# An encoder trunk with its first stage reordered, and the ALiBi bias applied by a scale in the softmax step

## The chip, the cores and the metric

One core of a Trainium2 chip runs the whole program. The metric is device time in microseconds, the median of the runs; all times below are microseconds (us) unless marked otherwise. PE is TensorE's matmuls, PEld its weight loads, DVE is VectorE, ACT is ScalarE, POOL is GpSimd, SP is SyncE, which here issues nearly all transfers.

## What is computed

Two layers over 512 tokens of width 1024. Each layer normalises the tokens with a scale and a shift from the conditioning vector, projects them (three dilated groups for 8 heads, a low-rank "latent" group for 8 more), runs dilated attention with ALiBi and latent attention, and then an MLP:

```python
c_act = jax.nn.silu(c)
for l in range(DEPTH):
    mod = c_act @ w_mod[l] + b_mod[l]
    sh1, sc1, gt1, sh2, sc2, gt2 = jnp.split(mod, 6, axis=-1)
    h = rms_norm(x, g_norm_mix[l]) * (1.0 + sc1[:, None]) + sh1[:, None]
    q_d, k_d, v_d, cq, ckv, k_rope = jnp.split(h @ w_in[l], cuts, axis=-1)
    q_d = rms_norm(q_d ..., g_q_dil[l]);  k_d = rms_norm(k_d ..., g_k_dil[l])
    o_dil = dilated_attention(q_d, k_d, v_d, positions, slopes)   # three windows, mixed
    o_mla = latent_attention(cq, ckv, k_rope, positions, ...)
    x = x + gt1[:, None] * (jnp.concatenate([o_dil, o_mla], axis=-1) @ w_out[l])
    h = rms_norm(x, g_norm_mlp[l]) * (1.0 + sc2[:, None]) + sh2[:, None]
    x = x + gt2[:, None] * (jnp.square(jax.nn.relu(h @ w_mlp_in[l])) @ w_mlp_out[l])

# inside each dilated window (dist = |pos_q - pos_k|, slope of head h = 2 ** -(h + 1)):
s = einsum(q, k) * Dh ** -0.5 - slopes * dist
s = where(mask, s, -1e30)
```

The kernel forms the three windows of a dilated head as one dense softmax over 512 keys: score plus a bias, where the bias is slope x |distance| plus a mask table of logarithms (`lnc`), both with their sign turned, so that the step takes a minimum.

## The kernel before

Every product runs in three matmuls of split operands (`mm3`: high x high, low x high, high x low). A weight tile is loaded by SP into `raw` (3 buffers) or `zz` (2 buffers), its high part is copied by ACT (L233) and its low part subtracted by POOL (L234). The tokens are tiled in eight feature tiles k (128 features by 512 tokens) and four token blocks tb.

The **first stage** (L734 to L793) makes the first projections. The 16 modulation blocks that it needs are loaded as 128x1024 weight tiles and multiplied on DVE with the broadcast conditioning vector `cb`, summing along the row (L170). The squares of x are added on DVE, summed by a matmul with ones (L753, `ones`), and turned into the inverse root `y` (`inv_rms`). Then, for each tile k: DVE multiplies x by the root into u (L759; L768 for the first), ACT makes the high half `h` (L772) and the full value (L773), and POOL or DVE the low half (L775, L763). PE takes for each tile the dilated group's 384 columns of all four token blocks and the latent group's 416 columns of all four. DVE's list alone is written out by hand there (`manual_schedule`); the others' orders come from the scheduler. Behind the loop stand the chains (squares L451, inverse roots, scaling L469), the transposes, the latent group's tail and rotary tables, and the distances (L327):

```python
for tb in range(4):
    W["do_chain"](tb, lbanks[tb])
for fn in PR[0]["tail"]:
    fn()
W["tail"]()
bias0 = distances()
```

Eight **stages** `st` follow, each with a pair of heads: 0 to 3 dilated, 4 to 7 latent. While the heads of one pair run (scores L492 and L493, softmax step L350, exponential, normalisation, transposes L365, values L377), `weave` puts the matmuls of the next pair's projections between them, each event at a position of the `TUNE` table. In layer 0 a dilated head makes its bias for each query block: ACT takes the absolute value of the signed distance times the slope (L345), POOL adds the mask table g (L346), SP stores it to HBM for layer 1, and DVE's softmax step adds it to the score:

```python
A.activation(b, dist[qb // 2][:, qb % 2], AF.Abs, scale=SLOPES[h])
G.tensor_tensor(b, b, g[:, 384 - 128 * qb:896 - 128 * qb], op=OP.add)
V.tensor_tensor_reduce(P, sc, b, op0=OP.add, op1=OP.min, scale=1.0, ...)
```

Names in the rows: `mm`, `sc`, `tr` are PSUM banks (4, 2 and 2 buffers); `qk`, `ot`, `pt`, `h`, `wh`, `wl`, `raw`, `zz`, `P`, `b`, `s`, `o` are SBUF buffers of a pool of that name; `kcol` and `mcol` are columns that scale keys.

## Time and profile before

| | us |
|---|---|
| runs | 1343.17, 1344.11, 1348.12; median 1344.11 |
| the profiled execution | 1343.71, its span 1341.6 |
| PE busy | 1263.8 (94%) |
| DVE, ACT, POOL busy | 762.4, 679.8, 652.0 |
| mean granted TensorE clock | 0.984 |

The profile follows one execution instruction by instruction. A timeline row gives the start, the duration, the engine, the line, the operation with output and inputs, and behind it in brackets how long the engine had been idle and what ended that. A row of grouped instructions gives busy time and the mean duration in ns. The granted clock is the share of full speed that TensorE had.

### The profile page before, as it was taken

The page shows a single profiled execution, that of the slowest core. Times are in us where ns is not written, and L with a number is a line of the kernel's source. Part 1 is how long each engine was busy: PE and PEld are TensorE (multiplying, and loading weights), DVE is VectorE, ACT ScalarE, POOL GpSimd, SP SyncE. Part 2 cuts the span into 40 slices and gives each one's busy share as a digit, 9 for nine tenths or more (in the row PEclk, how much of TensorE's full clock was granted, in tenths as well). Part 3 has the DMA queues.
Part 4 walks back from the last instruction along what each step waited for, and adds up shares of the span by engine and source line. Part 5 has one row for each costly group of instructions (what it writes and reads, how often), then busy time and mean ns, then how long its engine had stood idle before and what let it go on. Part 6 is the DMA issues. An engine that isn't in the chain of part 4 may idle for free.

```text
span 1341.6 us, 19641 instructions
## 1 busy us (share of the span) xinstructions
PE 1263.8 (94%) x7114; PEld 1108.2 (83%) x7114; DVE 762.4 (57%) x1644; ACT 679.8 (51%) x1421; POOL 652.0 (49%) x504
## 2 busy tenths in 40 slices
PE   4879988988999999999999999899899999999998
PEld 2878867877998888888899999798799888888888
DVE  6777797886763661834476678987672121121223
ACT  5567898777632322322237677887663232232321
POOL 5646876674534444444438333545452444444441
PEclk7989999999999999999999999999999999999999
DMA  9335543332254572844434244211121222232221
GB/s 340 113 100 174 184 156 110 105 122 69 79 176 166 192 250 95 278 166 161 166 121 131 77 135 123 86 48 63 40 72 64 95 95 96 96 106 96 94 95 64
DMA packets 57248, 167.62 MB, mean 125 GB/s; under 512 B 8640, under 2 KB 10816, under 8 KB 57152
## 3 DMA queue, kind: packets, MB, share of 16 engines
q1 hardware_dynamic: 57152, 166.38, 37.2%
q8 instruction: 56, 0.92, 0.3%
q14 instruction: 40, 0.33, 0.1%
HBM read 155.87 MB, written 10.49 MB: 124 GB/s over the span
## 4 chain that ended last, share of the span: by engine, by line
PE 75%; DVE 6%; ACT 5%; DMA 3%; POOL 3%; issue 2%; DVEq 0%; ACTq 0%; POOLq 0%
PE mm L241 22%; PE mm L244 22%; PE mm L245 22%; PE tr L377 3%; PE tr L365 2%; DMA raw<-in_wout_dram 1%; DVE pt L371 1%; POOL wl L234 1%; DVE P L350 1%; ACT P L354 1%; PE sc L241 1%; ACT wh L233 1%; POOL raw L167 1%; PE sc L244 1%; PE sc L492 1%
## 5 line engine op out<-in xcount | busy, mean ns | idle before, releaser
L234 POOL TENSOR_TENSOR wl<-raw,wh 128x1024 fp32r<-128x1024 f32 (+3 forms) x174 | 395.2, 2273 | 434.4 <-ACT wh L233 431.1
L233 ACT ACTIVATE wh<-raw 128x1024 fp32r<-128x1024 f32 (+3 forms) x174 | 174.7, 1004 | 264.7 <-PE mm L245 212.0
L670 DVE SCALAR_TENSOR_TENSOR x<-mm,mod,x 128x512 f32<-128x512 f32 (+1 forms) x152 | 92.4, 621 | 255.1 <-PE mm L245 254.5
L241 PE MATMUL mm<-h,wh 128*128 128x512 f32 (+1 forms) x544 | 198.3, 364 | 0.0
L244 PE MATMUL mm<-h,wl 128*128 128x512 f32 (+1 forms) x544 | 198.1, 364 | 0.0
L245 PE MATMUL mm<-h,wh 128*128 128x512 f32 (+1 forms) x544 | 197.9, 364 | 0.0
L241 PE MATMUL mm<-ot,wh 128*128 128x512 f32 (+1 forms) x416 | 147.1, 354 | 0.8 <-DVE x L670 0.4
L865 ACT ACTIVATE P<-mm 128x512 f32<-128x512 f32 (+1 forms) x80 | 41.0, 513 | 210.3 <-PE mm L245 206.8
L245 PE MATMUL mm<-ot,wh 128*128 128x512 f32 (+1 forms) x416 | 143.7, 349 | 1.5 <-POOL ot L663 1.5
L244 PE MATMUL mm<-ot,wl 128*128 128x512 f32 (+1 forms) x416 | 144.9, 349 | 0.0
L866 DVE SCALAR_TENSOR_TENSOR mm<-mm,P 128x512 f32<-128x512 f32 (+1 forms) x80 | 46.9, 589 | 135.7 <-ACT P L865 135.7
L241 PEld LDWEIGHTS mm<-h,wh 128*128 128x128 f32 x544 | 102.7, 189 | 16.3
L244 PEld LDWEIGHTS mm<-h,wl 128*128 128x128 f32 x544 | 102.7, 189 | 16.1
L245 PEld LDWEIGHTS mm<-h,wh 128*128 128x128 f32 x544 | 102.6, 189 | 16.2
L241 PE MATMUL mm<-qk,wh 128*128 128x512 f32 (+1 forms) x288 | 105.3, 366 | 1.0 <-DVE x L670 1.0
L244 PE MATMUL mm<-qk,wl 128*128 128x512 f32 (+1 forms) x288 | 105.3, 365 | 0.0
L245 PE MATMUL mm<-qk,wh 128*128 128x512 f32 (+1 forms) x288 | 105.2, 365 | 0.0
L170 DVE SCALAR_TENSOR_TENSOR pt<-pt,cb 128x1024 f32<-128x1024 f32 x56 | 100.7, 1828 | 0.0
L371 DVE TENSOR_TENSOR pt<-tr,pt 128x512 fp32r<-128x512 f32 x128 | 86.6, 684 | 18.1 <-ACT pt L370 17.5
L362 POOL TENSOR_SCALAR P<-P,hs 128x512 f32<-128x512 f32 x64 | 48.1, 751 | 99.9 <-DVE hs L355 81.0
L241 PE MATMUL mm<-wh,h 128*128 128x384 f32 x240 | 81.3, 353 | 11.7 <-ACT h L772 9.8
L365 PE MATMUL tr<-ident,P 128*128 128x128 f32 x512 | 77.5, 275 | 15.7 <-DVE o L381 6.1
(290 smaller groups left out, 2968.9 us busy)
## 6 DMA issues: line engine op xcount, KB each, us to landing
raw<-in_w_dram SPq DMA_DIRECT2D x64, 512.0 KB, 3.4
pt<-in_wmod_dram SPq DMA_DIRECT2D x56, 512.0 KB, 4.8
raw<-in_w2a_dram SPq DMA_DIRECT2D x48, 512.0 KB, 3.5
raw<-in_wmod_dram SPq DMA_DIRECT2D x24, 512.0 KB, 3.6
raw<-in_win_dram SPq DMA_DIRECT2D x30, 384.0 KB, 3.0
bias<-b SPq DMA_DIRECT2D x32, 256.0 KB, 2.1
raw<-in_wout_dram SPq DMA_DIRECT2D x16, 512.0 KB, 3.7
raw<-in_w2b_dram SPq DMA_DIRECT2D x16, 512.0 KB, 3.4
```

The costliest lines, as they stand in the source:

```text
L170: r = V.scalar_tensor_tensor(w, w, 1.0, cb, op0=OP.mult, op1=OP.mult, accum_out=out)
L233: ra = A.activation(hi, raw, AF.Copy)
L234: rg = G.tensor_tensor(lo, raw, f(hi), op=OP.subtract)
L241: r = T.matmul(out, sh, mh, start=first, stop=False)
L244: T.matmul(out, sl, mh, start=False, stop=False)
L245: T.matmul(out, sh, ml, start=False, stop=last)
L362: G.tensor_scalar(P, P, r_, 0.0, op0=OP.mult, op1=OP.add)
L365: T.transpose(tr[:, kc], P[:, kc * 128:(kc + 1) * 128], ident)
L371: V.tensor_tensor(lo, tr, f(hi), op=OP.subtract)
L670: V.scalar_tensor_tensor(xT[j][:, hf], p, gt[:, j:j + 1], xT[j][:, hf], op0=OP.mult, op1=OP.add)
L865: A.activation(r, p, AF.Relu)
L866: V.scalar_tensor_tensor(p, p, 0.0, r, op0=OP.max, op1=OP.mult)
```

## The change

It has three parts.

- **First stage.** c and the positions are loaded as rows and turned by PE. The squares are added in pairs by DVE for six tiles and not at all for two; five matmuls with ones accumulate the sum in PSUM. The broadcast of the conditioning vector stays in PSUM (`cbp`), and each modulation block is multiplied in two halves of 512. The small steps that make a tile's scale and shift go from ACT to DVE. POOL makes all eight low halves. The orders of SP, DVE, ACT and POOL are written out by hand.
- **Latent group.** In the k loop PE takes only the dilated group. The latent weights' second pair of tiles is loaded last (`late`); token blocks 0 and 1 are multiplied behind the dilated banks, blocks 2 and 3 inside the first stage of heads. The rotary tables move into stage 1, with the sine table and the reload of the exponential's table around the k loop.
- **Slope.** |distance| is made once, unscaled. Keys are multiplied by 1/slope (a small DVE step on the key's inverse root, `isl`), the mask table g is doubled in place by ACT at the start of every layer-0 dilated head (head h has half the slope of the one before it), and the softmax step multiplies the sum with the slope.

```diff
+    isl = col(8, "isl")
+    for h in range(8):
+        V.memset(isl[:, h:h + 1], 1.0 / SLOPES[h])
...
     def first_norm(j):
-        A.activation(modc[0][:, j:j + 1], mraw[:, j:j + 1], AF.Identity, bias=...)
-        A.activation(amix[0][:, j:j + 1], mraw[:, 8 + j:9 + j], AF.Identity, bias=gb0[:, j:j + 1], scale=...)
+        V.scalar_tensor_tensor(modc[0][:, j:j + 1], mraw[:, 0, j:j + 1], ..., mraw[:, 1, j:j + 1], op0=OP.add, op1=OP.add)
+        V.tensor_tensor(msum, mraw[:, 0, 8 + j:9 + j], mraw[:, 1, 8 + j:9 + j], op=OP.add)
+        V.scalar_tensor_tensor(amix[0][:, j:j + 1], msum, ..., gb0[:, j:j + 1], op0=OP.mult, op1=OP.add)
...
-    def inv_rms(p, v, y, t):
+    def inv_rms(p, v, t):
+        A.activation(t, p, AF.Ln, bias=epsc, scale=1.0 / D)
         V.tensor_scalar(v, p, 1.0 / D, EPS, op0=OP.mult, op1=OP.add)
-        A.activation(t, v, AF.Ln)
         A.activation(p, t, AF.Exp, scale=-0.5)
...
+    def distances(low):
         for qb in range(4):
             d = dist[qb // 2][:, qb % 2]
-            A.activation(d, row[:, 0], AF.Identity, bias=clm[:, 0, qb:qb + 1], scale=65536.0)
-            V.scalar_tensor_tensor(d, row[:, 1], clm[:, 1, qb:qb + 1], d, op0=OP.subtract, op1=OP.add)
+            if low:
+                V.scalar_tensor_tensor(d, rowf[:, 1], clm[:, 1, qb:qb + 1], d, op0=OP.subtract, op1=OP.add)
+                A.activation(d, d, AF.Abs)
+            else:
+                G.tensor_scalar(d, rowf[:, 0], 65536.0, clm[:, 0, qb:qb + 1], op0=OP.mult, op1=OP.add)
...
     def head(l, h, hd, score, bias, vals, o, hook=lambda at: None):
         pt = ...
+        if bias and l == 0:
+            A.activation(bias[1], bias[1], AF.Copy, scale=2.0)
...
-                    A.activation(b, dist[qb // 2][:, qb % 2], AF.Abs, scale=SLOPES[h])
-                    G.tensor_tensor(b, b, g[:, 384 - 128 * qb:896 - 128 * qb], op=OP.add)
+                    G.tensor_tensor(b, dist[qb // 2][:, qb % 2], g[:, 384 - 128 * qb:896 - 128 * qb], op=OP.add)
...
-                V.tensor_tensor_reduce(P, sc, b, op0=OP.add, op1=OP.min, scale=1.0, scalar=3e38, accum_out=m)
+                V.tensor_tensor_reduce(P, sc, b, op0=OP.add, op1=OP.min, scale=SLOPES[h], scalar=3e38, accum_out=m)
...
                     rs = rsqrt_tiny(v, 4 * nb, bank)
+                    rk = rs.rearrange("p (n k d) -> p n k d", k=2, d=2)[:, :, 1]
+                    V.tensor_tensor(rk, rk, isl[:, 2 * pr:2 * pr + 2]...to_broadcast([128, nb, 2]), op=OP.mult)
...
+            def late(i):
+                wr[4 + i] = load(a["winc"][0, i], 2 * W_C, ("raw", "zz")[i % 2])
+            def late_split(i):
+                W["put"](i, *split(wr[4 + i], 2 * W_C, ("ot", "ot") if i < 2 else ("wh", "wl")))
+            def mod_mul(i):
+                for w in range(2):
+                    c = slice(512 * w, 512 * w + 512)
+                    V.scalar_tensor_tensor(ml[i][:, c], ml[i][:, c], 1.0, cbp[w], ..., accum_out=mraw[:, w, i:i + 1])
+            with tc.manual_schedule(engines={E.SP, E.DVE, E.Activation, E.Pool}):
+                for k in range(8):
+                    mods(k)
+                    if k % 2 == 0:
+                        weights(k // 2)
+                    if k > 3:
+                        late(k - 4)
...
+                distances(False)
...
+                for k in range(8):
...
+                    V.tensor_tensor(u, xT[k], p, op=OP.mult)
+                    A.activation(hi, u, AF.Identity, bias=be, scale=ga)
+                    A.activation(u, u, AF.Identity, bias=be, scale=ga)
+                    G.tensor_tensor(lo, u, f(hi), op=OP.subtract)
+                    if k % 2 == 0 and k < 6:
+                        PR[0]["put"](k // 2 + 1, *split(wr[k // 2 + 1], 768))
                     if k < 7:
+                        mod_mul(9 + k)
+                        mod_mul(k + 1)
                         first_norm(k + 1)
+                    if k > 5:
+                        late_split(k - 6)
+                    for tb in range(4):
+                        PR[0]["step"](banks[tb][:, :384], k, tb)
...
             for tb in range(4):
                 PR[0]["do_chain"](tb, banks[tb])
+            gains()
+            for i in (2, 3):
+                late_split(i)
+            lbanks = {0: ps("sc")}
+            for k in range(8):
+                W["step"](lbanks[0][:, :W_C], k, 0, pin=k == 0)
+            distances(True)
...
+            if l == 0 and st == 0:
+                for tb in (2, 3):
+                    ev += spread(W["mm"][tb], 1.2 * tb - 2.4, 1.2 * tb - 1.3) + [(1.2 * tb - 1.25, W["chain"][tb])]
+                ev += [(2.5, W["tail"])] + flow(nx, 2.6, 7.6) + [(5.2, nx["tail"][0]), (8.8, nx["tail"][1])]
...
+            if l == 0 and st == 1:
+                ev += [(2, W["rope"])]
```

The order moves on several engines. On SP, in the first stage before, `winc` tiles (latent weights) come between modulation blocks (`wmod`) and the next pair's `win`:

```order
L165 DMA qk_495<-in_wmod_dram 128x1024
L165 DMA ot_499<-in_wmod_dram 128x1024
L232 DMA raw_404<-in_winc_dram 128x832
L506 DMA gr_730<-in_gqr_dram 128x32
L793 DMA cols_71<-in_cols_dram 128x71
L232 DMA raw_603<-in_win_dram 128x768
```

After, the last four `winc` tiles of the stage close the list of loads, and the fourth, `zz_227`, takes the buffer of the second, `zz_213`:

```order
L256 DMA zz_213<-in_winc_dram 128x832
L172 DMA qk_215<-in_wmod_dram 128x1024
L172 DMA qk_217<-in_wmod_dram 128x1024
L256 DMA zz_219<-in_win_dram 128x768
L256 DMA raw_221<-in_winc_dram 128x832
L172 DMA qk_223<-in_wmod_dram 128x1024
L172 DMA qk_225<-in_wmod_dram 128x1024
L256 DMA zz_227<-in_winc_dram 128x832
```

All latent weights are thus loaded late, the fourth last. On ACT, behind the eighth tile's value, before, there stands one weight copy (of the second pair) and then the squares and value copies of the dilated banks:

```order
L773 ACTIVATE pt_201<-pt_201,mod_167,am_169 128x512
L233 ACTIVATE wh_610<-raw_609 128x768
L451 ACTIVATE s_566<-mm_202 128x256
L457 ACTIVATE qk_564<-mm_202 128x2x64
L451 ACTIVATE s_566<-mm_203 128x256
L457 ACTIVATE qk_564<-mm_203 128x2x64
```

After, there stand three latent weight copies, a table load and four absolute values (the distances `ot_162` and `ot_163`) ahead of the same squares:

```order
L831 ACTIVATE pt_178<-pt_178,mod_143,am_145 128x512
L247 ACTIVATE ot_482<-zz_213 128x832
L112 ACT_TABLE_LOAD
L247 ACTIVATE wh_555<-raw_221 128x832
L247 ACTIVATE wh_559<-zz_227 128x832
L350 ACTIVATE ot_162<-ot_162 128x512 x2
L350 ACTIVATE ot_163<-ot_163 128x512 x2
L477 ACTIVATE s_511<-mm_279 128x256
```

The copy of `zz_227`, the last tile loaded, moved ahead of the squares. On PE, the first score of the first pair (`sc_785`), before, is followed by the next pair's projection (384 columns, `mm_819`):

```order
L547 MATMUL mm_722<-ident,zz_616 128x128
L492 MATMUL sc_785<-qk_562,qk_561 128x512
L493 MATMUL sc_785<-qk_563,qk_561 128x512
L241 MATMUL mm_819<-wh_604,h_184 128x384
L244 MATMUL mm_819<-wh_604,h_185 128x384
L245 MATMUL mm_819<-wl_605,h_184 128x384
```

After, the latent group's 416 columns of token block 2 (`mm_732`) stand around the two halves of that score:

```order
L521 MATMUL sc_699<-qk_507,qk_506 128x512
L265 MATMUL mm_732<-ot_462,h_164 128x416
L268 MATMUL mm_732<-ot_462,h_165 128x416
L269 MATMUL mm_732<-ot_463,h_164 128x416
L265 MATMUL mm_732<-ot_462,h_164 128x416
L268 MATMUL mm_732<-ot_462,h_165 128x416
L269 MATMUL mm_732<-ot_463,h_164 128x416
L522 MATMUL sc_699<-qk_508,qk_506 128x512
```

The latent transposes (L547) and the projection of the second pair stand further down.

More of the change, by code (lines that the diff above doesn't have):

```diff
@@ L146, in trunk @@
[L146 to L154 removed]
+        T.matmul(cbp[i], ones, dg.rearrange("p k c -> p (k c)"), start=True, stop=True)
@@ new lines, in trunk @@
+    sines = const.tile([128, 2, 4, 16], F32, name="sines")
+    sin, cos = sines[:, 0], sines[:, 1]
+    clm = const.tile([128, 3, 4], F32, name="clm")
+    parts = s2([4, 3, 128], tag="b")
+    V.tensor_copy(parts[:, 2], prow)
+    V.tensor_scalar(pi[:, 0], prow, 16, None, op0=OP.arith_shift_right)
+    V.tensor_scalar(pi[:, 1], prow, 65535, None, op0=OP.bitwise_and)
+    V.tensor_copy(parts[:, :2], pi)
+    turn = ps("sc")
+    for i in range(3):
+        T.transpose(turn[:, 4 * i:4 * i + 4], parts[:, i], ident[:4, :4])
@@ L238, in load_split, with load @@
         return hi, lo
+    def load(src, n, raw="raw", keep=False):
+        raw = t4(raw, [128, 1024], F32)[:, :n]
+        r = SY.dma_start(raw, src)
+        if keep:
+            tc.keep_in_program_order(r)
+        return raw
+    def load_split(src, n, keep=False, tags=("wh", "wl")):
+        return split(load(src, n, keep=keep), n, tags, keep=keep)
     def mm3(out, sh, sl, mh, ml, first, last, pin=False):
```

254 lines of the change are left out of this document (124 added, 130 removed).

## Prediction

> **What bounds the kernel now.** I read the page's table of busy tenths, then the busy time by stretches cut at the events that matter, then the timeline around those cuts.
>
> ```profile
> PE   4879988988999999999999999899899999999998
> ```
>
> ```profile
> 0.00:25.73 25.73, 5.86 (x6) 1.68 (x6) 14.81 (x43) 14.43 (x25) 11.55 (x20) 0.74 0.89 320
> 25.73:70.30 44.57, 39.82 (x192) 37.39 (x192) 33.71 (x46) 24.75 (x46) 28.67 (x23) 0.92 0.45 167
> 70.30:94.70 24.40, 17.46 (x77) 15.69 (x76) 19.86 (x52) 14.77 (x54) 6.75 (x8) 0.79 0.29 86
> 94.70:127.60 32.90, 30.02 (x187) 27.82 (x186) 24.61 (x61) 25.30 (x57) 23.82 (x17) 1.00 0.57 181
> 127.60:157.50 29.90, 28.07 (x171) 26.66 (x170) 25.05 (x60) 25.54 (x56) 23.93 (x17) 0.94 0.53 173
> 157.50:187.80 30.30, 28.02 (x186) 25.52 (x184) 26.39 (x66) 25.46 (x63) 19.90 (x17) 1.00 0.47 155
> 187.80:215.90 28.10, 20.66 (x130) 16.31 (x129) 18.94 (x56) 23.55 (x56) 25.98 (x28) 0.88 0.53 171
> ```
>
> The first row is PE in 40 slices of the span. Behind each stretch stand its length, then the busy time of PE, PEld, DVE, ACT and POOL, the granted clock, the DMA share and GB/s. After 216 us PE stands at nines and eights, so time can only come out of PE's idle or slow-clock time ahead of that: the first stage (to 94.7, the first softmax), and the four dilated stages behind it. The events of the first stage:
>
> ```profile
> 14.17 2.08 PE L753 MATMUL sc<-o,ones 128*128 128x512 f32 x2 [5.35 <-DVE o L128]
> 24.14 0.69 DVE L768 TENSOR_TENSOR pt<-x,P 128x512 f32<-128x512 f32 x1
> 53.26 0.62 PE L244 MATMUL mm<-wh,h 128*128 128x384 f32 x1 [1.87 <-POOL h L775]
> 54.00 0.52 PE L244 MATMUL mm<-wh,h 128*128 128x384 f32 x1
> 54.32 0.52 PE L245 MATMUL mm<-wl,h 128*128 128x384 f32 x1
> 56.62 0.43 PE L241 MATMUL sc<-wh,h 128*128 128x416 f32 x1
> 59.73 0.35 PE L241 MATMUL tr<-wh,h 128*128 128x416 f32 x1
> 59.79 0.81 ACT L772 ACTIVATE h<-pt,mod,am 128x512 fp32r<-128x512 f32 x1
> 59.91 0.35 PE L244 MATMUL tr<-wh,h 128*128 128x416 f32 x1
> 67.95 0.38 ACT L451 ACTIVATE s<-mm 128x256 f32<-128x256 f32 x1 [5.75 <-PE mm L245]
> 70.38 0.36 ACT L222 ACTIVATE st<-st,eps 128x8 f32<-128x8 f32 x1
> 79.60 0.47 PE L492 MATMUL sc<-qk,qk 128*128 128x512 f32 x1
> 92.94 2.98 POOL L346 TENSOR_TENSOR b<-b,ot 128x512 f32<-128x512 f32 x2 [6.93 <-ACT b L345]
> 94.70 0.68 DVE L350 CUSTOM_DVE_ANT_0 P<-sc,b 128x512 f32<-128x512 f32 x1
> 123.95 0.33 PE L241 MATMUL mm<-wh,h 128*128 128x384 f32 x1
> 124.12 0.33 PE L244 MATMUL mm<-wh,h 128*128 128x384 f32 x1
> 125.17 0.60 PE L365 MATMUL tr<-ident,P 128*128 128x128 f32 x4
> 125.52 1.19 PE L377 MATMUL tr<-pt,qk 128*128 128x256 f32 x8
> 126.55 0.40 PE L492 MATMUL sc<-qk,qk 128*128 128x512 f32 x1
> 126.78 0.40 PE L493 MATMUL sc<-qk,qk 128*128 128x512 f32 x1
> ```
>
> The first normalised tile is multiplied at 24.14; the eighth tile's high half comes at 59.79; the first score stands at 79.60, its softmax only at 94.70 (it waited for the bias), and the second pair's first score at 126.55. Start to start, a matmul of 384 columns costs 0.173 us, of 416 0.187, of 512 0.23, of 256 0.12 and a transpose 0.09; at the low clock, 384 columns cost 0.32 (54.00 to 54.32). That stretch came after a gap of only 1.87 and lasted from 53.26 to 56.62, so one such gap costs nearly half of 3.4, 1.6.
>
> **The sum is made in three terms** against the profiled execution (1343.71, its span 1341.6; the median of the runs shown is 0.4 higher). Anything within 0.5%, 6.7 us, is about what a measurement of this kernel can't tell from no change.
>
> **Term 1, the first stage, walked along the new order to the second pair's first score.** Durations of the rows it needs:
>
> ```profile
> L170 DVE SCALAR_TENSOR_TENSOR qk<-qk,cb 128x1024 f32<-128x1024 f32 x8 | 12.9, 1608 | 0.0
> L759 DVE TENSOR_TENSOR pt<-x,P 128x512 f32<-128x512 f32 x7 | 9.1, 1303 | 0.0
> 45.23 0.68 DVE L759 TENSOR_TENSOR pt<-x,P 128x512 f32<-128x512 f32 x1
> 45.84 1.21 DVE L170 SCALAR_TENSOR_TENSOR qk<-qk,cb 128x1024 f32<-128x1024 f32 x1
> 51.41 0.88 ACT L233 ACTIVATE wh<-raw 128x832 fp32r<-128x832 f32 x1
> 55.72 1.97 POOL L234 TENSOR_TENSOR wl<-raw,wh 128x832 fp32r<-128x832 f32 x1
> 65.94 1.28 POOL L775 TENSOR_TENSOR h<-pt,h 128x512 fp32r<-128x512 f32 x1
> 91.00 3.78 DVE L327 SCALAR_TENSOR_TENSOR ot<-pt,pc,ot 128x512 f32<-128x512 f32 x4
> raw<-in_win_dram SPq DMA_DIRECT2D x30, 384.0 KB, 3.0
> ```
>
> *Start.* The squares' five sums with ones cost 2.08 each at the low clock (10 us, behind two of the same kind for the broadcast), but VectorE is later: the first modulation block lands near 13.5, then come two blocks in halves (4 x 0.61), four distance steps (3.78), three small steps (0.5), and the inverse root (0.6 for v, 0.6 for the exponential, which overwrites what v reads, then 3 x 0.61). The first multiply starts near 22.3 (21 to 24), 1.8 earlier.
>
> *Per tile.* VectorE sets the pace: one multiply, four half blocks, and the three tiny steps that ACT did before (0.5). The multiply has both operands in SBUF; alone it took 0.61 start to start (45.23 to 45.84), its mean over seven was 1.30 with POOL at work 64% of the time (28.67 of 44.57). POOL's low half starts two ACT steps after it and a weight split follows every second tile, so I expect it to meet POOL less often: 0.95, between the two. Halves at 0.61 (below): 0.95 + 2.44 + 0.5 = 3.9 a tile; POOL's low half and half a split (1.28 + 0.9) fit. Seven tiles: 27.3, where before needed 24.14 to 52 and then lost 8 more on the last blocks. The eighth multiply starts at 49.6, its high half at 50.4 instead of 59.8.
>
> Why 0.61 for a half: the block of 1024 with two SBUF operands cost 1.21 alone, 1.61 in its mean; the softmax step at 94.70, with one operand in PSUM, cost 0.68 while POOL was at work. The broadcast now lies in PSUM, so I take the cheap end. Without that help a half costs 0.80, 28 of them 5.4 us more. The Trainium skill, "SBUF — State Buffer", "Who interferes with whom", says that a VectorE instruction with at most one SBUF input, outside its two-port modes, does not contend with GpSimd; by that rule the halves stay at 0.61, without it the sum is 5.4 higher. The trace agrees as far as it goes (0.68 with one operand in PSUM, 1.61 with none).
>
> *The hole.* The fourth late tile of the latent weights reuses the buffer of the second, so its load waits for POOL: low half of tile 8 done at 53.2, the second latent split at 55.2, landing 3.0 to 3.4 later (the last row), 58.4. ACT runs its list in order, and this tile's copy stands ahead of the four absolute values, the squares of all four banks, the mask's scaling and two more splits. So ACT stands still from about 55.5 to 58.4 with finished banks behind it, then: copy 0.9, four absolutes 2.1, squares and copies 1.7 (67.95 to 70.38 less a split of 0.74), scaling 0.9, splits 1.5, logarithm near 65.5. Transposes begin 2.5 later and take 4; 24 latent matmuls (4.5) stand ahead of the first score, and PE is at the low clock again after 5 us of rest, 1.6 more by the rows above: first score at 77.6, 2.0 earlier. The Trainium skill, "TensorE: Matmul & The Clock Gate", Part 1, lets the clock fall only after about 3.4 us without work and rise after as much of steady work; this hole is long enough for that too, 1.7 by its figure, and the trace disagrees on the fall (1.87 sufficed).
>
> *What moved behind the first score.* To the second pair's first score PE has now 141 matmuls of 384 columns, 48 of 416, 60 transposes, 32 of 256 and 16 scores: 24.4 + 9.0 + 5.4 + 3.8 + 3.7 = 46.3; before, 139, 0, 57, 24 and 16: 24.0 + 5.1 + 2.9 + 3.7 = 35.7, in 46.95 (79.60 to 126.55), so it lost 11.3, most of it because the bias was late (POOL's row at 92.94). Now the bias is ready when the score is. Behind the bias PE idled 2.9 of 32.9 (94.70 to 127.60); over 46 us that is 4.1, and I leave 4.5 for it, since the last latent blocks and the first softmaxes now share VectorE. 77.6 + 46.3 + 4.5 = 128.4, with 1.3 more matmul time done than before at that point: worth 127.1 against 126.55. **Term 1 is +0.5**: what ends 9 us earlier is paid back by the hole and by 9 us of latent matmuls that used to fill PE's waiting in the old first stage. Its bounds: -5.9 if the multiplies never meet POOL (2.4) and the hole closes (4.0: the load and part of the clock); +8.3 with the multiplies at 1.30 (2.4) and the halves at 0.80 (5.4).
>
> **Term 2, the bias in the four dilated stages.**
>
> ```profile
> L345 ACT ACTIVATE b<-ot x30: 612/621/672, 96.6 to 210.8; 128x512 f32<-128x512 f32 x30
>   POOL b L346: 7.8, 10
> ```
>
> ```profile
> 50.00:90.00 40.00, 6.21 (x14) 0.87 0.25 75
> ```
>
> The first line is ACT's scaled absolute per query block, the second what POOL waited for it, and the single line POOL's busy time with the rotary tables (6.21, 14 instructions; then clock and DMA). 32 absolutes (17 us of ACT at 0.53 start to start) go; 8 scalings of the 896-wide mask (0.9 each, 7.2) and four absolutes come. POOL's 7.8 us of waiting go, but up to 6.2 of rotary work, which lay beside a waiting POOL before, move into the second pair's stage, where POOL is busy 23.93 of 29.90. PE idled 1.8 + 2.3 + 7.4 in the three stages after 127.6; in the last, POOL is the queue that is full. Between 1.6 (7.8 less 6.2) and 7.8 I take **-4.0**, below the middle for the rotary work; in the last stage nothing is added to the full queue.
>
> **Term 3**: 24 small multiplications of the key's factor by 1/slope, 0.16 to 0.2 each on VectorE: the 16 of layer 1 lie in chains with PE's matmuls of the next block above them; **+0.2**, up to 3.2 if none were covered. The score, softmax and transposes keep their instructions, the scale of the softmax step being an immediate.
>
> Sum: 1343.7 + 0.5 - 4.0 + 0.2 = 1340.4.
>
> **Rivals.** (a) The dilated stages gain more: with ACT's hop gone the head pipeline closes most of PE's 11.5 idle us, and the hole is short. For it: POOL waited ten times for ACT. Against: POOL 190 to 203 never waits. -5.9 and -7.8: 1343.7 - 13.7 + 0.2 = 1330.2 at the far end, 1337 at the near one. (b) Slower, by one mechanism: the mask is scaled in place at each head's start, on ACT, in order, behind POOL's last addition of the head before (1.3), which itself waits for the store of the block two before (2.1 to landing). If POOL is more than one exponential behind, ACT stands 2.4 at each of eight heads with the normalisations queued behind it; if half reaches PE (8 x 1.2) and the 4.0 don't come: 1343.7 + 0.5 + 9.6 + 0.2 = 1354. It decides once ACT's idle time before the scaling passes about 1.5 us a head. (c) The operand in PSUM doesn't help and the multiplies meet POOL as before: +5.4 + 2.4, 1348.2. Against it stands the softmax step's 0.68; I count it inside the forecast's band.
>
> **Chances.** Forecast, within 0.5%, rival (c) with it: 0.51, its own range 1337 to 1349. Rival (a), faster by more: 0.35. Rival (b): 0.14. The low end, 1331, is just above (a)'s far end; the high end, 1351, leaves out most of (b).
>
> **What the new profile would show.** Right: the first multiply near 22.3 and 3.6 to 4.2 between multiplies; ACT idle until the DMA of the fourth latent tile near 58; first score near 77, first softmax within 2 us of it; second pair's first score near 128. POOL's waits for ACT's bias gone. Wrong: a pace above 4.5 per tile; no idle ACT ahead of the squares; the second pair before 123 (then rival (a)); ACT idle ahead of the mask's scaling by over 10 us in all (then (b)).

## The result and the profile after

The changed kernel took 1375.08 us (median of four runs, 1373.52 to 1376.98) against 1343.64 before (1342.96 to 1348.12): a ratio of 1.0227 [1.0201, 1.0254], slower by 31.4. The forecast was 1340.4, no change, in a range that ended at 1351. The profiled execution took 1376.98, its span 1375.2.

The page's busy times, PE's 40 slices and the granted clock in the same slices:

```profile
PE 1280.0 (93%) x7126; PEld 1120.1 (81%) x7126; DVE 773.4 (56%) x1727; ACT 668.1 (49%) x1379; POOL 648.5 (47%) x511
PE   4787786998999999999999999999899999999999
PEclk8889988999999999999999999999999999999999
```

PE is busy 16.2 us longer than the 1263.8 of before, for twelve instructions more, and idle 95.2 instead of 77.8. So about half of the 33.6 by which the spans differ, 17.4, is idle PE. Of the other half about 3 us are work: busy time times the mean granted clock (0.984 before, 0.974 after) grew by that much, and ahead of the first multiply PE has 18 instructions where it had 6. The remaining 13 or so are matmuls at a lower clock. Both rows above are low in the first seven slices, 241 us. The stretch up to the first multiply, the one up to the first score, and the stages of pairs 1 to 3, each cut at the first score of a pair (columns as in the prediction's stretches), after:

```profile
0.00:23.17 23.17, 9.17 (x18) 3.79 (x18) 16.97 (x61) 9.87 (x15) 8.11 (x22) 0.95 0.85 316
23.17:82.66 59.49, 42.13 (x161) 36.34 (x162) 45.59 (x117) 31.57 (x58) 29.78 (x20) 0.76 0.47 168
82.66:144.00 61.34, 51.61 (x299) 49.16 (x298) 36.23 (x86) 32.57 (x84) 27.52 (x19) 0.92 0.32 110
144.00:186.96 42.96, 31.43 (x179) 28.84 (x179) 30.38 (x65) 24.38 (x53) 26.09 (x30) 0.84 0.41 139
186.96:213.59 26.63, 24.86 (x161) 23.02 (x160) 21.54 (x57) 19.81 (x48) 17.88 (x16) 1.00 0.34 116
```

and before, cut at the same events from the first multiply on:

```profile
24.14:79.60 55.46, 44.24 (x212) 40.82 (x212) 43.12 (x70) 32.46 (x76) 32.14 (x24) 0.89 0.47 170
79.60:126.55 46.95, 42.02 (x237) 39.20 (x237) 35.59 (x89) 33.19 (x82) 27.11 (x22) 0.93 0.45 142
126.55:156.64 30.09, 28.26 (x172) 26.76 (x170) 25.24 (x60) 25.11 (x56) 23.07 (x17) 0.94 0.50 162
156.64:186.32 29.68, 27.40 (x180) 24.91 (x179) 25.80 (x64) 24.40 (x60) 19.28 (x16) 1.00 0.47 155
```

The first score comes 3.1 later, the second pair's 17.5 later, the third pair's 30.3 later and the fourth's 27.3 later. The delay is 31.7 at the first layer's MLP and 35.0 at the second's (at their first relu). Two stages carry most of it: pair 1's (61.34 for 46.95) and pair 2's (42.96 for 30.09, for nearly the same number of matmuls).

**The k loop**, timeline of after (ACT, DVE, POOL and SP at its beginning and end):

```profile
23.17 0.69 DVE L829 TENSOR_TENSOR pt<-x,sc 128x512 f32<-128x512 f32 x1
25.63 1.28 POOL L832 TENSOR_TENSOR h<-pt,h 128x512 fp32r<-128x512 f32 x1 [2.01 <-ACT pt L831]
26.33 0.59 DVE L208 SCALAR_TENSOR_TENSOR mod<-mraw,cols 128x1 f32<-128x1 f32 x1
26.86 1.82 POOL L248 TENSOR_TENSOR wl<-zz,wh 128x768 fp32r<-128x768 f32 x1
27.03 1.67 DVE L211 SCALAR_TENSOR_TENSOR am<-msum,cols,gb 128x1 f32<-128x1 f32 x1
28.62 0.67 DVE L829 TENSOR_TENSOR pt<-x,sc 128x512 f32<-128x512 f32 x1
...
45.94 1.82 POOL L248 TENSOR_TENSOR wl<-zz,wh 128x768 fp32r<-128x768 f32 x1
47.78 0.33 SPq L256 DMA_DIRECT2D zz<-in_winc_dram  x1
57.27 0.67 DVE L829 TENSOR_TENSOR pt<-x,sc 128x512 f32<-128x512 f32 x1
62.55 0.88 ACT L247 ACTIVATE wh<-zz 128x832 fp32r<-128x832 f32 x1
65.41 0.36 ACT L477 ACTIVATE s<-mm 128x256 f32<-128x256 f32 x1
82.66 0.39 PE L521 MATMUL sc<-qk,qk 128*128 128x512 f32 x1
```

A step of one column (L211), 0.2 us of work, took 1.67: it started 0.17 behind POOL's weight split and ended when the split did. The step at 26.33 ended in the same way with POOL's low half. The next multiply, and with it the next tile, came behind them. The long step repeats at 36.64, 46.09 and 55.53, behind every split of the loop.

**Pair 1's stage**, its last ten us:

```profile
127.63 0.84 ACT L247 ACTIVATE wh<-raw 128x768 fp32r<-128x768 f32 x1 [2.37 <-DMA raw<-in_win_dram]
128.38 0.16 ACT L239 ACTIVATE mm<-st 128x8 f32<-128x8 f32 x1
129.01 2.42 DVE L182 SCALAR_TENSOR_TENSOR raw<-raw,cb 128x1024 f32<-128x1024 f32 x1
132.26 0.86 DVE L493 TENSOR_TENSOR st<-st,isl 128x4 f32<-128x4 f32 x1
133.16 1.29 DVE L498 TENSOR_TENSOR zz<-mm,st 128x512 f32<-128x512 f32 x2
134.00 0.66 PE L508 MATMUL mm<-ident,zz 128*128 128x128 f32 x2 [7.12 <-DVE zz L498]
```

PE stood still for 7.12 until the second pair's last scaled keys came. The exponential of their inverse root on ACT (L239) stood behind the copy of a weight tile that had not landed; then came a modulation block beside POOL's split (2.42, where one at 154.30 took 1.24), and the key's step by 1/slope (0.86, where the shortest took 0.15).

**Pair 2's stage**, around its middle:

```profile
153.58 0.32 POOL L540 TENSOR_TENSOR rot<-sines,gr 128x64 f32<-128x64 f32 x1
157.18 2.81 POOL L248 TENSOR_TENSOR wl<-raw,wh 128x768 fp32r<-128x768 f32 x1
160.02 0.81 SPq L256 DMA_DIRECT2D raw<-in_win_dram  x2
163.50 0.84 ACT L247 ACTIVATE wh<-raw 128x768 fp32r<-128x768 f32 x1 [2.66 <-DMA raw<-in_win_dram]
167.79 1.11 PE L389 MATMUL tr<-ident,P 128*128 128x128 f32 x4 [4.28 <-DVE o L405]
169.09 4.58 DVE L182 SCALAR_TENSOR_TENSOR raw<-raw,cb 128x1024 f32<-128x1024 f32 x1
176.16 1.12 PE L389 MATMUL tr<-ident,P 128*128 128x128 f32 x4 [5.28 <-ACT P L382]
```

The rotary tables stand on POOL among the weight splits, so the splits come later; loads wait for the buffers that the splits free, ACT waits for the loads, and PE stands still twice, for 4.28 and 5.28. A modulation block beside POOL's work from 169.0 to 172.6 took 4.58.

### The profile page after: what moved, and what is told of

It is laid out like the page before. It is cut to its first block, busy times and chain, and to the rows that moved or that the text cites. A ratio compares the mean times of both kernels' runs of the same rounds, so it can differ in the third digit from the quotient of the medians.

```text
span 1375.2 us, 19672 instructions
## 1 busy us (share of the span) xinstructions
PE 1280.0 (93%) x7126; PEld 1120.1 (81%) x7126; DVE 773.4 (56%) x1727; ACT 668.1 (49%) x1379; POOL 648.5 (47%) x511
## 4 chain that ended last, share of the span: by engine, by line
PE 74%; DVE 9%; ACT 5%; POOL 4%; issue 4%; DMA 3%; SPq 0%; POOLq 0%; DVEq 0%; ACTq 0%
PE mm L265 21%; PE mm L268 21%; PE mm L269 21%; PE tr L401 3%; PE tr L389 2%; POOL wl L248 2%; DVE qk L789 1%; DVE raw L182 1%; DMA raw<-in_wout_dram 1%; PE sc L265 1%; DVE pt L395 1%; PE sc L268 1%; PE sc L269 1%; ACT wh L247 1%; PE mm L667 1%
## 5 line engine op out<-in xcount | busy, mean ns | idle before, releaser
L248 POOL TENSOR_TENSOR wl<-raw,wh 128x1024 fp32r<-128x1024 f32 (+2 forms) x173 | 393.9, 2280 | 450.1 <-ACT wh L247 447.3
L247 ACT ACTIVATE wh<-raw 128x1024 fp32r<-128x1024 f32 (+2 forms) x173 | 173.6, 1005 | 266.8 <-PE mm L269 210.3
L268 PE MATMUL mm<-ot,wl 128*128 128x512 f32 (+1 forms) x416 | 144.7, 348 | 0.0
L268 PEld LDWEIGHTS mm<-h,wl 128*128 128x128 f32 x544 | 102.7, 189 | 16.2
L389 PE MATMUL tr<-ident,P 128*128 128x128 f32 x512 | 80.4, 284 | 21.3 <-DVE o L405 9.4
L265 PE MATMUL mm<-wh,h 128*128 128x384 f32 (+1 forms) x252 | 86.8, 362 | 14.0 <-ACT h L830 13.8
L268 PE MATMUL mm<-wh,h 128*128 128x384 f32 (+1 forms) x252 | 90.8, 361 | 6.4 <-POOL h L832 6.3
```

What stands on the lines that cost most here:

```text
L247: ra = A.activation(hi, raw, AF.Copy)
L248: rg = G.tensor_tensor(lo, raw, f(hi), op=OP.subtract)
L265: r = T.matmul(out, sh, mh, start=first, stop=False)
L268: T.matmul(out, sl, mh, start=False, stop=False)
L389: T.transpose(tr[:, kc], P[:, kc * 128:(kc + 1) * 128], ident)
```

## The experiments

Each ratio is to the kernel before on the same chip, with its 95% interval. A time given as above or below another kernel is a difference of medians, and across chips it is uncertain by some 3 us: there the medians of the kernel before are 1343.64 to 1346.63. Counted from the kernel before on the same chip, what is given below as 8.1, 6.5, 4.2 and 19.6 under the changed kernel is 9.5, 7.9, 7.2 and 22.6, and the 7.1 over it is 5.7. The numbers given with a kernel beside its time are the first scores of pairs 1, 2, 3 and 4 (before: 79.6, 126.6, 156.6, 186.3; after: 82.7, 144.0, 187.0, 213.6).

### The parts apart

**Slope part alone, on the kernel before.**

```diff
+            A.activation(d, d, AF.Abs)
...
+        if bias and l == 0:
+            A.activation(bias[1], bias[1], AF.Copy, scale=2.0)
...
-                    A.activation(b, dist[qb // 2][:, qb % 2], AF.Abs, scale=SLOPES[h])
-                    G.tensor_tensor(b, b, g[...], op=OP.add)
+                    G.tensor_tensor(b, dist[qb // 2][:, qb % 2], g[...], op=OP.add)
...
+                    V.tensor_tensor(rk, rk, isl[...], op=OP.mult)
```

> The kernel before with the slope part alone: |distance| once and unscaled, keys times 1/slope, the mask doubled at each head's start, the softmax step's scale. Theory: the loss of 31 us lies in the first stage's new order and in the work that it pushes behind the first score, and the slope part is small: 1339 to 1346 us, with POOL's waits for ACT's bias gone. Rival: the slope part is what hurts (small key multiplication held up beside POOL, ACT waiting for POOL at each head's start): 1350 us or more.

1362.58, 1.0131 [1.0116, 1.0146]: +17.5, where the forecast had -3.8 (81.1, 127.2, 164.3, 193.6). **The changed kernel without it** (the same lines, the other way round):

> The changed kernel with the slope part taken back: the absolute with the slope per query block on ACT, the mask as loaded, no multiplication of the keys. Theory (slope part small): 1371 to 1379 us. Rival (slope part hurts): 1362 us or less. If both this and the slope part alone are slow, the two hurt separately; if both are fast, only together.

1372.29, 1.021 [1.0194, 1.0225]. So the first stage with the latent move costs 27.3 by itself, the slope part 17.5 by itself, and both together 31.4: they don't add up. Both lengthen pair 2's stage, which takes 30.1 before, 37.1 with the slope part alone, 42.7 without it and 43.0 with both; that this is the whole reason is not shown.

**The rotary tables one stage later**, in the changed kernel:

```diff
-            if l == 0 and st == 1:
+            if l == 0 and st == 2:
                 ev += [(2, W["rope"])]
```

> The changed kernel with the rotary tables in the third pair's stage instead of the second's. Theory: the tables on POOL hold up the weight split and the modulation block of the second stage, and with them PE (idle 4.3 and 5.3 us there at 167.8 and 176.2): the third pair's first score comes some 8 to 11 us earlier than 186.96 and the time falls to 1364 to 1369 us, unless the third stage pays the same. Rival: the weight loads are late there for another reason (buffers that come free late), and the tables only stand beside it: 1372 us or more.

1367.01, 1.0162 [1.0147, 1.0177], 8.1 below the changed kernel. Pair 2's stage takes 29.2 (144.7 to 173.9) instead of 43.0, and part of that is given back in pair 3's (30.0 instead of 26.6).

**The small steps with one operand in PSUM**, in the changed kernel:

```diff
+    cps = ps("sc")
+    V.tensor_copy(cps[:, 0:8], cols[0][:, C_BMOD:C_BMOD + 8])
+    V.memset(cps[:, 8:16], 0.0)
+    V.tensor_copy(cps[:, 16:24], gb0)
...
-        V.tensor_tensor(msum, mraw[:, 0, 8 + j:9 + j], mraw[:, 1, 8 + j:9 + j], op=OP.add)
+        V.scalar_tensor_tensor(msum, mraw[:, 0, 8 + j:9 + j], mraw[:, 1, 8 + j:9 + j], cps[:, 8:9], ...)
-        V.scalar_tensor_tensor(amix[0][:, j:j + 1], msum, ..., gb0[:, j:j + 1], ...)
+        V.scalar_tensor_tensor(amix[0][:, j:j + 1], msum, ..., cps[:, 16 + j:17 + j], ...)
```

> The changed kernel with one operand of each of the three small steps (the tile's shift and scale) in PSUM, nothing else changed. Theory: a VectorE step with all operands in SBUF stands until the running POOL instruction ends, so the small step at 27.03, 36.64, 46.09 and 55.53 took 1.7 us instead of 0.2; with an operand in PSUM it takes 0.2, the eighth multiply starts near 50.5 instead of 57.27, and the time falls by 4 to 7 us, to 1368 to 1371. Rival: the step waits for something else (a result that is late, or the row's accumulated sum): its 1.7 us stay and so does the time, 1373 to 1377.

1368.54, 1.017 [1.0153, 1.0187], 6.5 below the changed kernel (75.1, 136.6, 177.8, 204.3). The last small step of a tile by its line (count, shortest, median and longest in ns, first and last start), after and here:

```profile
L211 DVE SCALAR_TENSOR_TENSOR am<-msum,cols,gb x8: 204/944/1822, 19.5 to 55.5; 128x1 f32<-128x1 f32 x8
```

```profile
L215 DVE SCALAR_TENSOR_TENSOR am<-msum,cols,sc x8: 203/215/216, 19.5 to 49.2; 128x1 f32<-128x1 f32 x8
```

The same work at the same place takes 0.2 throughout, and the eighth multiply starts at 49.35 instead of 57.27. This shows that the three tiny steps, with all operands in SBUF, were what stretched the k loop.

**The halves with the broadcast in SBUF**, in the changed kernel, to take the PSUM operand away:

```diff
+        A.activation(cb[:, 512 * i:512 * i + 512], cbp[i], AF.Copy)
...
-                    V.scalar_tensor_tensor(ml[i][:, c], ml[i][:, c], 1.0, cbp[w], ...)
+                    V.scalar_tensor_tensor(ml[i][:, c], ml[i][:, c], 1.0, cb[:, c], ...)
...
-            for i in range(2):
-                tc.keep_in_program_order(A.activation(cb[:, 512 * i:512 * i + 512], cbp[i], AF.Copy))
```

> The changed kernel (1375.1 us) with the modulation halves reading the broadcast from SBUF instead of PSUM; all else the same. Theory: a half with two SBUF operands stands while a POOL instruction runs; POOL works 3.1 us of each 5.4 us pair of tiles, so the eighth multiply comes 2 to 6 us later than 57.27 and the time is 1377 to 1382. The small steps may then meet POOL less, which takes some of it back. Rival: 0.61 us a half is its cost wherever the operand lies: 1373 to 1377, and no half over 0.7.

1382.18, 1.0271 [1.0243, 1.0298], 7.1 above the changed kernel. The halves by their line, and two rows of this kernel's timeline:

```profile
L790 DVE SCALAR_TENSOR_TENSOR qk<-qk,cb x32: 674/682/977, 14.3 to 57.7; 128x512 f32<-128x512 f32 x32
26.16 1.79 POOL L833 TENSOR_TENSOR h<-pt,h 128x512 fp32r<-128x512 f32 x1 [2.01 <-ACT pt L832]
26.87 1.09 DVE L209 SCALAR_TENSOR_TENSOR mod<-mraw,cols 128x1 f32<-128x1 f32 x1
```

The halves hardly lengthen (median 0.682 instead of 0.676). It is POOL's low half, started just behind one of them, that does (1.28 to 1.79), and the small step behind it (0.59 to 1.09): in these rows whichever of the two engines comes second waits. The eighth multiply starts at 61.40 instead of 57.27.

### The slope part, in pieces (on the kernel before)

**The key's step with its operand in PSUM.**

```diff
-                    V.tensor_tensor(rk, rk, isl[...], op=OP.mult)
+                    rs = rsqrt_tiny(v, 4 * nb, bank, unslope)   # multiplies y, in the bank, by isl
```

> The slope part alone (1362.6 us), with the multiplication by 1/slope made on the key's raw inverse root in PSUM instead of on the finished one in SBUF; same number of steps. Theory: that small step, with both operands in SBUF, stands until POOL's instruction ends (0.56 to 1.3 us instead of 0.16) and all that follows in the chain with it; in layer 1, where nothing else of the part is left, it is the 3 to 4.6 us between the first softmax and the MLP. Then 1355 to 1359. Rival: the step costs its 0.16 and layer 1's loss comes from elsewhere: 1361 or more.

1356.23, 1.0087 [1.006, 1.0115], 6.4 below the slope part alone. **The absolute value per query block kept on ACT**, unscaled:

```diff
-            A.activation(d, d, AF.Abs)
+                    A.activation(b, dist[qb // 2][:, qb % 2], AF.Abs)
+                    G.tensor_tensor(b, b, g[...], op=OP.add)
```

> The slope part alone, but with ACT's absolute per query block kept (unscaled, into the bias buffer, POOL adds the mask in place, as before). Theory: with the absolute gone POOL's additions stand further forward in POOL's list and wait there themselves for the softmax that frees one of two bias buffers (21.7 us in nine waits from 125 to 216), with weight splits and normalisations queued behind; with ACT's step back most of layer 0's 14 us goes: 1347 to 1353. Rival: layer 0 loses by the small key multiplication and the mask's doubling, which are still there: 1359 or more.

1355.49, 1.0082 [1.0061, 1.0102], 7.1 below it. **No doubling of the mask table:**

```diff
-            A.activation(bias[1], bias[1], AF.Copy, scale=2.0)
```

This kernel leaves the mask as loaded, so its masked weights differ, and only its time is of use.

> The slope part alone without the doubling of the mask at each head's start (the mask stays as loaded, so masked weights differ). Theory: ACT does not wait there (no idle time ahead of the doubling in the trace) and eight times 0.9 us lie beside other work: 1359 to 1363. Rival (the prediction's way to slower): ACT stands behind POOL at each head's start, the normalisations behind it: 1352 or less without it.

1358.71, 1.0109 [1.0083, 1.0135], 3.9 below it. The three savings, 6.4, 7.1 and 3.9, add up to about the 17.5. That doesn't make them separate prices: a pass over the mask costs 10.0 by itself (below), and taking it out here gives back 3.9. The key's step by its line in the changed kernel, and with the operand in PSUM (where two more of the 24, written to `sc`, took at most 0.17):

```profile
L493 DVE TENSOR_TENSOR st<-st,isl x24: 150/164/1486, 71.1 to 859.0; 128x2 f32<-128x2 f32 x16, 128x4 f32<-128x4 f32 x8
```

```profile
L476 DVE TENSOR_TENSOR mm<-mm,isl x22: 156/169/171, 72.8 to 843.3; 128x2 f32<-128x2 f32 x14, 128x4 f32<-128x4 f32 x8
```

Its median is what the forecast priced; single ones cost nine times that. In layer 1, from its first softmax to its MLP's first relu, it is 247.2 before, 250.5 with the slope part and 247.4 here, 3.1 less. Where the rest of the 6.4 lies the profile doesn't show: its execution took 1360.43, 4.2 above this kernel's median. POOL's longest waits between 125 and 216 us, before, with the slope part alone, and with the absolute values kept:

```profile
POOL P L362 <- DVE hs L355: 14.1, 5, 8.0
POOL b L346 <- ACT b L345: 6.6, 7, 1.8
```

```profile
POOL b L352 <- DVE hs L356: 21.7, 9, 5.0
```

```profile
POOL P L368 <- DVE hs L361: 13.1, 6, 4.5
POOL b L352 <- ACT b L351: 5.5, 6, 2.2
```

The waits for ACT's absolute values went, as forecast, and POOL waits as long as before, now ahead of the addition itself and for the softmax. That this holds up the splits queued behind it is read from the list; shown is only that the removal cost 7.1. None of the 7.1 is back at the fourth pair's first score (193.9 with the absolute values kept, 193.6 with the slope part alone); 4.9 of it is at the MLP's first relu (366.8 instead of 371.7). So these waits, most of them ahead of that score, aren't shown to be what cost it. **A pass over the mask table that changes nothing**, on the kernel before, shows what the pass costs by itself:

```diff
+        if bias and l == 0:
+            A.activation(bias[1], bias[1], AF.Copy, scale=1.0)
```

> The kernel before with one thing added that computes nothing: at each layer-0 dilated head's start ACT copies the mask onto itself (scale 1.0, 8 times 0.9 us). Theory: the scheduler remakes the lists of all engines around an added step, and the positions of weight loads and projections, which fitted the old lists, no longer do: 1347 to 1352 us, with PE's waits in other places than before. Rival: the step lies beside other work and the lists' new order is as good as the old: 1342 to 1346.

1355.7, 1.0067 [1.0042, 1.0091]: 10.0 between the medians, for eight instructions that ACT's groups between 70 and 250 us show thus (total, mean ns, then ACT's idle time ahead of them):

```profile
L336 ACT ACTIVATE ot<-ot 128x896 f32<-128x896 f32 x8 | 7.6, 950 | 0.3 <-POOL b L349 0.3
```

ACT waits 0.3 in all for POOL, and 1.6 in all ahead of the eight doublings of the changed kernel. So rival (b)'s mechanism is not what costs here, though the price is as large as its 9.6.

### Loads, latent work and the late bias

**Two of pair 3's four weight loads behind pair 1's stage**, in the changed kernel, so that the exponential no longer stands behind ACT's late copy:

```diff
-                ev += spread(PR[st + 2]["load"], tn("LD0"), tn("LD1"))
+                if l == 0 and st == 0:
+                    ev += spread(PR[2]["load"][:2], tn("LD0"), 6.3) + spread(PR[2]["load"][2:], 9.9, 9.95)
...
```

> The changed kernel (1375.1 us) with the third and fourth weight tile of the third pair loaded behind the last chain of the first stage of heads, so that ACT's exponential of that chain no longer stands behind a copy that waits for its transfer. Theory: PE's wait of 7.1 us before 134.0 shrinks to about 4 (the modulation block on VectorE stays in the chain), the second pair's first score comes at 140 to 141.5 instead of 144.0, and the time falls to 1370 to 1373. Rival: the tiles are needed so soon afterwards that the wait moves behind the second pair's first score: 1374 to 1378.

1375.32, 1.0213 [1.0196, 1.0229]: pair 2 started 2.9 earlier (141.1), the fourth pair 2.6 (211.0), and the layer's MLP 1.4. In the medians nothing of it is left; counted from the kernel before on the same chip it is 2.7, about what can't be told from none. **The latent blocks 2 and 3 ahead of the heads:**

```diff
-            for tb in range(2):
+            for tb in (2, 3):
+                lbanks[tb] = ps("mm")
+                for k in range(8):
+                    W["step"](lbanks[tb][:, :W_C], k, tb)
+            for tb in range(4):
                 W["do_chain"](tb, lbanks[tb])
+            W["tail"]()
...
-            if l == 0 and st == 0:
-                for tb in (2, 3):
-                    ev += spread(W["mm"][tb], 1.2 * tb - 2.4, 1.2 * tb - 1.3) + [(1.2 * tb - 1.25, W["chain"][tb])]
...
```

> The changed kernel with the latent group's token blocks 2 and 3, its chains and transposes ahead of the first score instead of between the first heads, and the next pair's projection where it stood before. Theory: the 9 us of latent matmuls are paid wherever they stand once they have left the k loop, where PE idles; the first score comes near 93, the second pair's first score at 140 to 144, the time is 1370 to 1376. Rival: it is their place among the heads that costs (VectorE shared, weight buffers free late): 1367 or less.

1370.91, 1.0184 [1.0163, 1.0206], 4.2 below the changed kernel (91.5, 137.6, 171.2, 200.8): the first score comes 8.8 later, pair 1's stage shrinks from 61.3 to 46.1, and most of that is lost again later.

**The kernel before with its bias early.** The forecast put 11.3 us of loss down to the late bias; so the distances go right behind `gains()`, with the eighth low half on VectorE:

```diff
-                            G.tensor_tensor(lo, u_of(k + 1), f(hi), op=OP.subtract)
+                            (V if k == 6 else G).tensor_tensor(lo, u_of(k + 1), f(hi), op=OP.subtract)
...
+            bias0 = distances()
             for tb in range(4):
                 PR[0]["do_chain"](tb, banks[tb])
...
-            bias0 = distances()
```

> The kernel before with two moves and nothing of the change: the eighth tile's low half on VectorE (idle from 59.4) instead of behind three weight splits on POOL (65.94), and the distances ahead of the chains instead of last. Theory: PE gets the eighth tile 4 to 5 us earlier, the first softmax comes near 82 instead of 94.7, and the time falls to 1334 to 1339, below both kernels. Rival: the earlier bias only moves PE's waits into the heads of the first pair, as most of what the change made earlier was lost: 1341 to 1345.

1356.75, 1.0072 [1.005, 1.0093] (81.0, 129.6, 167.8, 200.1). The first softmax starts at 82.7 instead of 94.7, and the second pair 3.1 later all the same: the first pair's stage takes 48.6 where it took 46.95. **The low half alone** (the first two lines of that diff):

> The kernel before with the eighth tile's low half on VectorE (idle from 59.4) instead of on POOL (65.94, behind three weight splits), nothing else. Theory: PE gets that tile 4 to 5 us earlier and the time falls to 1338 to 1341. Rival: the first stage does gain, and the stages behind it lose as much in the remade lists (as when the distances were moved too, 1356.8): 1344 to 1352.

1354.41, 1.0052 [1.0034, 1.007]. The first score comes 3.8 earlier, pair 2 6.2 and pair 3 2.5; then pair 3's stage takes 38.92, with 18 matmuls more in it than before (the profile is of an execution of 1348.6, 5.8 below this kernel's median):

```profile
154.13:193.05 38.92, 32.66 (x198) 29.39 (x197) 28.58 (x68) 29.09 (x67) 24.45 (x19) 0.91 0.50 161
```

### Put together, and what is left

**Three mended**: rotary tables later, small steps and key's step with an operand in PSUM (the three edits above, in the changed kernel).

> The changed kernel with three things mended together: rotary tables in the third pair's stage (alone -8.1 us), an operand of the small steps in PSUM (alone -6.5), the multiplication by 1/slope on the raw inverse root in PSUM (alone -6.4 on the other base, at least layer 1's 3). Theory: they are separate losses and add up: 1375.1 - 8.1 - 6.5 - 3 to -6 = 1354 to 1358. Rival: they are seen through the same idle PE time, and one hides the other: 1361 or more.

1355.51, 1.0065 [1.0046, 1.0084] (73.5, 134.2, 162.4, 192.3): 19.6 back, about the sum of the three (8.1, 6.5, and the 6.4 that the key's step was worth on the kernel before: 21.0). **Five mended**, with the absolute values per block and the latent blocks ahead as well:

> The changed kernel with five things mended: the three of the mended kernel (1355.5 us), ACT's absolute per query block (alone -7.1 on the slope part), and the latent blocks 2 and 3 ahead of the first score (alone -4.2). Theory: what is left of the 31 us lies in these two: 1342 to 1348, the level of before. Rival: what is left is the latent work that the k loop no longer hides, and that stays: 1350 to 1356.

1354.42, 1.0052 [1.0034, 1.007]: what gave 7.1 on the slope part and 4.2 on the changed kernel gives 1.1 on top of the three. **The first stage mended, without the slope part:**

> The changed kernel without the slope part, its rotary tables in the third pair's stage and its small steps with an operand in PSUM. Theory: the new first stage alone, mended, is still slower than the old one, since 9 us of latent matmuls have left a loop in which PE idles: 1353 to 1358 (1372.3 - 8.1 - 6.5 = 1357.7). Rival: the slope part costs here what it costs alone beyond its small step, 11 us, and without it the mended stage is level with before: 1343 to 1348.

1353.53, 1.0057 [1.0039, 1.0074] (70.6, 129.8, 158.4, 195.4): its first score is 9.0 earlier than before's, its second pair 3.3 later. The three mended kernel, which is this one with the slope part and its key's step mended, takes 2.0 more, within what the chips differ by: there the rest of the slope part, its pass over the mask included, costs next to nothing.

Three mended versions, the idle pass and the moved low half all lie near 1355. Perhaps any remade list costs that much, before's being a lucky one. Two kernels take the kernel before, keep every instruction, and only let the scheduler place some otherwise. **One place:** POOL's eighth low half ahead of a weight split, the splits and all else kept where they stood.

```diff
+                            r = G.tensor_tensor(lo, u_of(k + 1), f(hi), op=OP.subtract)
+                            if k == 6:
+                                tc.keep_in_program_order(r)
...
             for fn in PR[1]["load"][:2]:
-                fn()
+                fn(keep='pool')
```

> The kernel before with the eighth tile's low half one place further forward in POOL's list, ahead of a weight split of the second pair (1.84 us); every other instruction of every engine stands where it stood. Theory: with the lists kept a local gain reaches the end: the low half comes at 64.1 instead of 65.94, the first score 1 to 2 us earlier, and the time falls by 1 to 2 us, 1342 to 1344. Rival: even so the stages behind it give it back, or lose more: 1345 or more.

1345.68, 0.9999 [0.9987, 1.001]. The low half stood 1.8 earlier and the first score 0.3. **Same work**, with the low half and the rotary tables' products kept in program order:

```diff
-            G.tensor_tensor(C[:, :, 0], cos, ga, op=OP.mult)
+            tc.keep_in_program_order(G.tensor_tensor(C[:, :, 0], cos, ga, op=OP.mult))
...
```

> The kernel before with the same instructions, but the rotary tables' multiplications held in the order of the program, so that the scheduler remakes the lists of VectorE, ACT and POOL (some 13% of their rows stand elsewhere, PE's list is nearly the same). Theory: remade lists alone cost 3 to 12 us, as the idle pass did: 1348 to 1357. Rival: an order is as good as another when the work is the same, and the idle pass cost by its own 7 us of ACT: 1343 to 1347.

1346.72, 1.0002 [0.999, 1.0014]. Compared row by row with the trace of the kernel before, up to the first layer's MLP 13% of POOL's rows stand elsewhere, but only 3% of DVE's, 4% of ACT's and 1% of PE's; behind it they are 17, 29, 23 and 10%. So POOL's list remade in part in layer 0, and all four in part behind it, cost nothing. This leaves the question open for layer 0: up to the MLP the idle pass has 26% of PE's rows, 32% of DVE's and 35% of ACT's elsewhere.

**What stays open** is these last 10 us. In the profiles of the idle pass, the low half, five mended and the stage without slope, pair 3's stage takes 36.8 to 38.9 instead of 29.7. The moved low half is not in that stage at all, the rotary tables (in two of the four) and the idle pass are; in three mended, which has the rotary tables there too, it takes 29.9, and what follows up to the MLP pays 6.3 instead. Whether the remade order of PE, DVE and ACT costs the time or the added steps do, the runs don't separate. No version beat the kernel before.

## Why the prediction was wrong

Three steps of the sum failed. The small VectorE steps were priced by their size, in Term 1 (0.5 a tile) and in Term 3 (0.2 in all); they waited out GpSimd instructions instead and cost 6.5 and (on the kernel before) 6.4. Term 2 took a removed wait for a gain and put nothing down for the eight passes over the mask. And it charged the moved rotary tables by POOL's time alone; they cost 8.1. Mended together, the small steps, the key's step and the tables give back 19.6 of the 31.4. The cause of the last 10 stays open. No rival reached 1375 either: the highest, (b), stood at 1354.

- **Start**: 22.3 forecast, 23.17 measured, inside its bounds. The terms listed for it add up to 23.25; the slip was in the adding.
- **Halves**: 0.61 each from start to start, right. The Trainium skill, "SBUF — State Buffer", "Who interferes with whom", says that a VectorE instruction with at most one SBUF input, outside its two-port modes, does not contend with GpSimd; the trace agrees, 0.672 to 0.684 in all 32, also in those at 25.60 and 31.04 that ran beside POOL's low half. But the other price, 0.80 with both operands in SBUF, was wrong: the halves stayed at 0.682, and the loss came through POOL's low half and the small step behind it.
- **Per tile**, the term that was mis-sized first: small steps at 0.5 a tile. They took 0.5 to 0.9 without a split beside them and 2.3 to 2.5 with one. The multiply, priced at 0.95 for two operands in SBUF, took 0.6: in the changed kernel the root that it reads lies in PSUM (`sc` in its rows), which the prediction overlooked. The eighth came at 57.3, not 49.6. The small steps have all operands in SBUF; the prediction looked for waits beside POOL at the wide halves and not at the tiny steps. With one operand of theirs in PSUM the eighth multiply stood at 49.35.
- **The hole** did not occur. SP issued the fourth late tile's load at 47.78, when POOL ended the split of 45.94: it took that tile's buffer, not that of the second latent tile, as stands above at the list of loads. ACT's copy at 62.55 waited for nothing. The slow k loop put the first score at 82.7 instead of 77.6 (whose steps, as listed, add up to 78.1).
- **Behind the first score**: 50.8 forecast, 61.3 measured. PE's work was counted about right: 46.3 at full speed, and 51.6 busy at a clock of 0.92 is 47.5. But 4.5 for idle time was too little for the 9.7 that came, of which one wait alone was 7.1. The reason given was wrong as well: an early bias gained the kernel before nothing (its second pair came 3.1 later).
- **Term 2** had the wrong sign: -4.0 forecast, and the slope part alone with Term 3 costs 17.5. The 7.8 of waiting that went was time in which POOL's list stood anyway; with the slope part alone it stood as long for the softmax. The 6.2 of rotary work was counted as POOL time, at most 6.2 of loss; moved into that stage it cost 8.1, by splits that came late and loads behind them. The eight passes over the mask, 7.2 of ACT's time, stood in the sum at nothing: alone they cost 10.0, out of the slope part 3.9, and in the mended kernel next to nothing; what decides this is open.
- **Term 3**: 0.2, at most 3.2; it cost 6.4. The count was right and the duration was not: up to 1.49 beside POOL, in a chain that PE waits for.
- **The clock** was priced once, at 1.6. Of the 16.2 by which PE's busy time grew, about 13 is the lower clock, beside 17.4 more of idle time: the idle time of the k loop and of pair 1's and 2's stages was paid for nearly twice. The granted clock between the first multiply and the first score was 0.76, against 0.89 before.
- **The rivals**: the gain of (a) did not come. (b)'s price came, and without its mechanism: ACT waited 1.6 in all at the mask table, where it was to pass 10. (c)'s condition did not hold, since with the operand in PSUM no multiply or half was held up beside POOL; that taking it away cost 7.1 where 5.4 was priced is luck, for the halves themselves did not lengthen.

## What to carry over

Price a tiny VectorE step by what GpSimd runs beside it, not by its size: with all operands in SBUF it waited out whole GpSimd instructions here, and one operand in PSUM freed it. A wait that an engine is relieved of is worth nothing if the next thing in its list waits as long for something else that is late; look past the removed wait before counting it. Where PE's gaps come in a train, price the clock with them: here 17.4 more of idle time went with about 13 more in slower matmuls.

## What the runs showed of the chip

A VectorE step of 128x1 with all operands in SBUF took 0.20 alone and 1.67 to 1.82 behind a GpSimd split. With VectorE's halves reading both operands from SBUF, GpSimd's low half of 1.28 became 1.79.

The clock fell without any long gap. Three stretches of the k loop after (busy times and clock as above), and the row behind the longest gap in them:

```profile
30.00:40.00 10.00, 5.76 (x25) 4.49 (x26) 9.93 (x29) 4.32 (x7) 4.34 (x3) 0.95 0.97 362
40.00:50.00 10.00, 8.10 (x28) 7.09 (x28) 9.86 (x27) 4.56 (x6) 4.33 (x3) 0.66 0.14 48
50.00:58.00 8.00, 5.83 (x22) 4.94 (x20) 7.81 (x20) 2.50 (x5) 4.48 (x3) 0.79 0.32 116
```

```profile
39.84 0.97 PE L265 MATMUL mm<-wh,h 128*128 128x384 f32 x4 [1.60 <-ACT h L830]
```

PE idled 4.2 of the first ten us, in gaps of at most 1.6, and still ran at 0.95; in the next ten it was at 0.66, needing 8.10 for 28 instructions where 25 had taken 5.76. In these three rows the clock goes with the idle time of the stretch before (4.2, then 1.9); more than that three rows can't show.
